# Attention's numerators in two single PSUM banks, and its output gates in three one-tile buffers

## The chip, the cores and the metric

The kernel runs on one core of a Trainium2 chip. The metric is the device time of one execution in microseconds (us). The engines are named as the profile names them: PE is TensorE (PEld its weight loads), DVE is VectorE, ACT is ScalarE, POOL is GpSimd, and SP is the engine whose queue issues the DMAs here.

## The reference

One layer of a hybrid decoder is computed for a prompt of 1024 new tokens and, beside it, for 8 sequences of 4 tokens each that go on from stored states. The branch that the change touches is an mLSTM with 4 heads of width 512, worked in chunks of 128 tokens:

```python
s = jnp.einsum('bhtd,bhsd->bhts', qc, kc) * d
num = jnp.einsum('bhts,bhse->bhte', s, vc) + g[..., None] * jnp.einsum('bhtd,bhde->bhte', qc, c)
den = jnp.sum(s, axis=-1) + g * jnp.einsum('bhtd,bhd->bht', qc, n)
h = num / jnp.maximum(jnp.abs(den), jnp.exp(-m_t))[..., None]
...
c_new = decay[..., None, None] * c + jnp.einsum('bhsd,bhse->bhde', kw, vc)
...
hc = hc.transpose(0, 2, 1, 3) * jax.nn.sigmoid(o_pre.astype(jnp.float32)).reshape(B, S, N_HEADS, HEAD_DIM)
hc = head_rmsnorm(hc, mlstm_norm_w).reshape(B, S, MLSTM_WIDTH).astype(x.dtype)
bm = (hc * jax.nn.silu(m_z)) @ w_mlstm_down
```

So each token tile's numerators are divided by a denominator, multiplied by the output gate `o`, normalised, and multiplied by a second gate `z`.

## The kernel before, in words

**Stages.** First the input projection of all heads is made, and q, k, v, the output gate (after its sigmoid) and z (after its silu) go to DRAM (`qkD`, `vD`, `oD`, `zD`). Then attention (`attn`) runs as a generator that is fed between the matmuls of the merge gates (`merge_gates`, whose products are the `mm` tiles). Behind it the decoding sequences (`sample`) run in the same way between the matmuls of the pooling branch, and the down projections (`downs`) and the tail end the kernel. Every fp32 product is made of three matmuls of a high and a low part (`mm3`, lines 383 to 385). A scheduler orders each engine's instructions: the first in program order that its own timing says is ready goes first. So matmuls of the merge gates, which stand among the steps of attention, fill waits of attention as long as there are any left.

**Attention** goes through 16 pairs of token tiles (4 heads of 4 pairs, numbered 0 to 15 here; pairs 0, 4, 8 and 12 are the first of a head, have no state yet and so fewer matmuls). For a pair the loads of `v`, `o` and `zz` (the gate z) bring 128 partitions x 2 tiles x 512 columns each, 512 KB, into one buffer for each of the three. For each of its two tiles:

- The numerators `num` are formed in two PSUM banks of one tile with one buffer: 256 columns of values in either bank, and in columns 256 and 257 of the first the denominator. The matmuls with the state's parts `Ch`, `Cl` go d by d, both banks for each d, and then those with the scores `ph`, `pl` and the values `vhi`, `vlo`.
- `attn_rows` reads them: ACT takes the denominator's absolute value (L1047), DVE makes its reciprocal (L1048, L1049), and DVE multiplies both banks by it and by `o`, in place of `o`, in one instruction of 512 columns (L1051). With that the banks are free. ACT sums the squares (L1054), the root is made on DVE and POOL (L391, L393), and DVE multiplies by it and by z (L1056).
- k is transposed and scaled into `kh`, `kl`.

Then the state C gets its update, 8 products `kv` in two PSUM buffers (L1025 or L1027 on DVE, then the split into `Ch`, `Cl`). The scores of the next pair are prepared among these (`attn_ahead`). At the pair's end `attn_turn` transposes both tiles of `o` on PE (L1063) and sends them off. Since `o` has one buffer, the next pair's `o` is loaded when these transposes are done; the buffer of `zz` is free when the second tile's L1056 is.

SP issues nearly all DMAs, in order: one that waits for its buffer holds those behind it.

Of the kernel before, what the change touches and what calls it, by code (L numbers as in the profile page):

```python
# [12 lines left out]
AF = mybir.ActivationFunctionType  # L13
ALU = mybir.AluOpType
# [4 lines left out]
P = 128  # L19
# [3 lines left out]
NS = DB * DS  # L23
NT = T + NS
H, DH = 4, 512
M = H * DH
KT = D // P
L = 128
# [312 lines left out]
class Trunk:  # L341
# [631 lines left out]
    def attn(self):  # L973

        nc = self.nc
        a = self.atp
# [3 lines left out]
        cut = lambda x: ((0, x[:, 0, :]), (1, x[:, 1, :256]))  # L980
        vh, vl = self.vhi, self.vlo
        for n, (h, j) in enumerate(pairs):
            qk, qh, ql, ph, pl = made
            both = lambda x: x[h][2 * j * L:(2 * j + 2) * L, :].rearrange("(i p) n -> p i n", p=P)
            r0 = h * NCH + 2 * j
            v, o, z = [self.t(a, [P, 2, 512], x) for x in ("v", "o", "zz")]
            for x, src in ((v, self.vD), (o, self.oD), (z, self.zD)):
                nc.sync.dma_start(x, both(src))
            khl = []
            for i in range(2):  # L990
                t = slice(i * L, (i + 1) * L)
                num = self.t(self.ps, [P, 2, 512], "num")
                outs = (num[:, 0, :258], num[:, 1, :256])
                if j:
                    for d in range(4):
                        for (x, mh), (_, ml) in zip(cut(self.Ch[:, d]), cut(self.Cl[:, d])):
                            self.mm3(outs[x], qh[:, d, t], ql[:, d, t], mh, ml, d == 0, False)
                v3 = v[:, i].rearrange("p (a n) -> p a n", a=2)
                self.hi(vh[i][:, :, 0:256], v3)
                self.lo(vl[i][:, :, 0:256], v3, vh[i][:, :, 0:256])  # L1000
                for b in range(i + 1):
                    c = slice((i + b) * L, (i + b + 1) * L)
                    for (x, mh), (_, ml) in zip(cut(vh[b]), cut(vl[b])):
                        self.mm3(outs[x], ph[:, c], pl[:, c], mh, ml, j == 0 and b == 0, b == i)
                yield True
                self.attn_rows(r0 + i, num, o[:, i], z[:, i])
                ps = self.miscps()
                for d in range(4):
                    nc.tensor.transpose(ps[:, d * P:(d + 1) * P], qk[:, 4 + d, t], self.ident)
                kh = self.t(a, [P, 4, P], f"kh{i}", F32R)  # L1010
                kl = self.t(a, [P, 4, P], f"kl{i}", F32R)
                ps3 = ps.rearrange("p (d f) -> p d f", d=4)
                w_s = self.tok[:, 1, r0 + i:r0 + i + 1]
                self.hi(kh, ps3, w_s)
                self.lo(kl, ps3, kh, w_s)
                khl.append((kh, kl))
                yield True
# [19 lines left out]
            for i in range(2):  # L1037
                self.attn_turn(h, 2 * j + i, o[:, i])
            if j == NCH // 2 - 1:
# [3 lines left out]
    def attn_rows(self, r, num, o, z):  # L1043

        nc, a = self.nc, self.atp
        den = self.t(a, [P, 1], "den", bufs=2)
        nc.scalar.activation(den, num[:, 0, 256:257], AF.Abs)  # L1047
        nc.vector.tensor_scalar(out=den, in0=den, scalar1=self.tok[:, 2, r:r + 1], scalar2=None, op0=ALU.max)  # L1048
        nc.vector.reciprocal(den, den)  # L1049
        o3 = o.rearrange("p (a n) -> p a n", a=2)  # L1050
        nc.vector.scalar_tensor_tensor(out=o3, in0=num[:, :, 0:256], scalar=den, in1=o3, op0=ALU.mult, op1=ALU.mult)  # L1051
        ss = self.t(a, [P, 1], "ss", bufs=2)
# [27 lines left out]
    def sample(self):  # L1080
# [57 lines left out]

        num = self.t(self.ps, [P, 2, 512], "num")
        qm = self.t(a, [P, 132 * DB], "qm")  # L1140
        nc.gpsimd.memset(qm, 0.0)
        for h in range(H):
# [19 lines left out]
            for b in range(DB):  # L1162
# [4 lines left out]
                for d in range(4):  # L1167
                    nc.tensor.matmul(num[32 * d:32 * d + 32, 0, :], lhsT=qm[:, b * P + d * NS:b * P + (d + 1) * NS], rhs=ct[:, d, :],  # L1168
                                     start=b == 0, stop=b == DB - 1)
# [8 lines left out]
            nsb = self.t(a, [P, DH], "voz", bufs=3)  # L1178
            nc.scalar.activation(nsb, num[:, 0, :], AF.Copy)
            nc.tensor.matmul(num[32 * h:32 * h + 32, 1, :], lhsT=self.sel, rhs=nsb, start=True, stop=False)  # L1180
        vo = []
        for src in (self.vSD, self.oSD, self.zSD):
            x = self.t(a, [P, DH], "voz", bufs=3)
            nc.sync.dma_start(x, src.rearrange("h t e -> (h t) e"))
            vo.append(x)
        nc.tensor.matmul(num[:, 1, :], lhsT=pb, rhs=vo[0], start=False, stop=True)
        hc = self.t(a, [P, DH], "shc")
        nc.vector.scalar_tensor_tensor(out=hc, in0=num[:, 1, :], scalar=dn, in1=vo[1], op0=ALU.mult, op1=ALU.mult)
        ss = self.t(a, [P, 1], "sss")
# [4 lines left out]
        for d in range(4):  # L1194
            nc.tensor.transpose(ps[:, d * P:(d + 1) * P], hc[:, d * P:(d + 1) * P], self.ident)
        for h in range(H):
            nc.vector.tensor_copy(self.hcS[:, h], ps.rearrange("p (d h t) -> p h d t", d=4, h=H)[:, h])
# [148 lines left out]
    def downs(self, first):  # L1346
# [35 lines left out]
        self.mmov = []  # L1382
        self.ms = self.t(self.cp, [P, KT, NS], "ms")
        for g in range(4):
# [163 lines left out]
    def run(self):  # L1548
# [50 lines left out]
        self.cp2, _c2 = self.pool("const2")  # L1599
        self.hcS = self.t(self.cp2, [P, H, 4, NS], "hcS")  # L1600
        self.wp, _w = self.pool("weights2")
# [77 lines left out]
```

## Time and profile before

| | |
|---|---|
| Median of 3 runs | 2232.88 us (2228.46 to 2236.81) |
| Profiled execution, its own time | 2232.33 us |
| Span of the profile (first to last instruction) | 2230.6 us |
| Mean granted clock of TensorE | 0.99 |
| Busy: PE / DVE / ACT / POOL | 97% / 56% / 40% / 6% |

The profile is of one execution. Idle time of an engine is put down to what released the instruction behind it. A granted clock of 1.00 is 2.4 GHz, and 0.50 is 1.2 GHz. Attention's matmuls start near 980 us of the span and end near 1345 us.

### The profile page before, as it was taken

To read this page: it belongs to the slowest core of one execution; us is meant where nothing else is said; L and a number is where in the kernel's file an instruction comes from. 1 tells how busy PE (TensorE), PEld (TensorE's weight loads), DVE (VectorE), ACT (ScalarE), POOL (GpSimd) and SP (SyncE) were. 2 spreads that over 40 slices of the span, in tenths; PEclk is the share of its full clock that TensorE was granted. 3 is DMA by queue.
4 is the path that set the end of the run, shared out by engine and by line. 5 is a ranking of instruction groups with operands and counts; after the bars stand their busy time and mean duration, and the time that the engine had idled before them with its cause. 6 is when DMAs were issued, how large, how long until landed. Compare 5 with 4: busy or idle time off the path is not lost.

```text
span 2230.6 us, 40176 instructions
## 1 busy us (share of the span) xinstructions
PE 2159.6 (97%) x16407; PEld 2054.8 (92%) x16407; DVE 1257.2 (56%) x2172; ACT 900.8 (40%) x1791; POOL 122.7 (6%) x335
## 2 busy tenths in 40 slices
PE   7999999999999999899999899999988999999998
PEld 6899999999999999899999798787778999999998
DVE  6855576456746565446566675576563243543645
ACT  5645455444635353633333343222223331213443
POOL 1100001000101000000000100000000000000000
PEclk9999999999999999999999999999999999999999
DMA  4233333333233331675655645887774343323112
GB/s 153 85 107 108 102 103 96 108 102 115 93 107 96 112 93 38 195 245 160 196 158 161 204 140 175 294 289 261 252 265 162 97 139 102 108 97 104 53 48 83
DMA packets 238601, 312.72 MB, mean 140 GB/s; under 512 B 13994, under 2 KB 170066, under 8 KB 238416
## 3 DMA queue, kind: packets, MB, share of 16 engines
q1 hardware_dynamic: 238416, 310.15, 42.8%
q8 instruction: 129, 2.11, 0.4%
q14 instruction: 56, 0.46, 0.1%
HBM read 200.01 MB, written 110.45 MB: 139 GB/s over the span
## 4 chain that ended last, share of the span: by engine, by line
PE 87%; DMA 6%; DVE 3%; ACT 2%; SPq 1%; issue 1%; POOL 0%; DVEq 0%; POOLq 0%; ACTq 0%
PE mm L221 21%; PE mm L163 14%; PE mm L383 12%; PE mm L385 12%; PE mm L384 12%; PE num L1168 2%; PE misc L953 2%; PE num L383 1%; PE kv L383 1%; PE num L384 1%; PE num L385 1%; PE kv L384 1%; PE kv L385 1%; PE kv L1172 1%; DMA o<-oD 1%; DMA ct<-state_mlstm_C 1%
## 5 line engine op out<-in xcount | busy, mean ns | idle before, releaser
L376 DVE TENSOR_TENSOR wlo<-wraw,whi 128x1024 fp32r<-128x1024 f32 (+1 forms) x220 | 238.7, 1086 | 228.7 <-ACT whi L370 222.9
L370 ACT ACTIVATE whi<-wraw 128x1024 fp32r<-128x1024 f32 (+1 forms) x220 | 209.2, 951 | 340.8 <-PE mm L221 107.1
L383 PE MATMUL mm<-hh,whi 128*128 128x352 f32 (+1 forms) x832 | 265.7, 319 | 14.5 <-ACT sz L1311 9.0
L385 PE MATMUL mm<-hh,wlo 128*128 128x352 f32 (+1 forms) x832 | 262.6, 316 | 0.0
L384 PE MATMUL mm<-hl,whi 128*128 128x352 f32 (+1 forms) x832 | 261.7, 315 | 0.0
L221 PE MATMUL mm<-wlo,hh 128*128 128x256 f32 x768 | 216.1, 281 | 0.0
L221 PE MATMUL mm<-whi,hl 128*128 128x256 f32 x768 | 215.9, 281 | 0.0
L221 PE MATMUL mm<-whi,hh 128*128 128x256 f32 x768 | 214.6, 279 | 0.0
L383 PEld LDWEIGHTS mm<-hh,whi 128*128 128x128 f32 x832 | 158.8, 191 | 28.5 <-ACT sz L1311 11.3
L384 PEld LDWEIGHTS mm<-hl,whi 128*128 128x128 f32 x832 | 159.2, 191 | 5.7 <-issue 4.4
L385 PEld LDWEIGHTS mm<-hh,wlo 128*128 128x128 f32 x832 | 158.7, 191 | 5.5 <-issue 4.2
L323 DVE SCALAR_TENSOR_TENSOR z<-z,vcols,z 128x556 f32<-128x556 f32 x192 | 146.8, 794 | 8.4 <-ACT z L321 6.6
L163 PE MATMUL mm<-hh,whi 128*128 128x264 f32 x512 | 148.4, 290 | 1.0 <-DVE z L179 0.6
L163 PE MATMUL mm<-hl,whi 128*128 128x264 f32 x512 | 146.2, 286 | 0.4 <-DVE hl L376 0.3
L163 PE MATMUL mm<-hh,wlo 128*128 128x264 f32 x512 | 145.5, 284 | 0.0
L221 PEld LDWEIGHTS mm<-whi,hh 128*128 128x128 f32 x768 | 144.7, 188 | 0.0
L221 PEld LDWEIGHTS mm<-whi,hl 128*128 128x128 f32 x768 | 144.6, 188 | 0.0
L221 PEld LDWEIGHTS mm<-wlo,hh 128*128 128x128 f32 x768 | 144.3, 188 | 0.2
L1173 DVE SCALAR_TENSOR_TENSOR ct<-ct,dec,kv 128x512 f32<-128x512 f32 x128 | 93.4, 744 | 70.9 <-PE kv L1172 61.3
L385 PE MATMUL mm<-mvhB,wlo 128*128 128x352 f32 x384 | 123.2, 322 | 0.0
L384 PE MATMUL mm<-mvlB,whi 128*128 128x352 f32 x384 | 123.0, 322 | 0.0
L383 PE MATMUL mm<-mvhB,whi 128*128 128x352 f32 x384 | 122.1, 324 | 0.0
(462 smaller groups left out, 6071.6 us busy)
## 6 DMA issues: line engine op xcount, KB each, us to landing
wraw<-w_in SPq DMA_DIRECT2D x112, 512.0 KB
ct<-state_mlstm_C SPq DMA_DIRECT2D x32, 1024.0 KB
new_C_sample<-ct SPq DMA_DIRECT2D x32, 1024.0 KB
qkD<-z SPq DMA_DIRECT2D x64, 256.0 KB
qk<-qkD SPq DMA_DIRECT2D x16, 1024.0 KB
sgD<-sz SPq DMA_DIRECT2D x16, 528.0 KB
sg<-sgD SPq DMA_DIRECT2D x16, 528.0 KB
vD<-z SPq DMA_DIRECT2D x32, 256.0 KB
```

Of the source, the lines that this page charges most:

```text
L163: self.tr.nc.tensor.matmul(ps[:, j, :CH], lhsT=st[:, k], rhs=mv[k][:, c], start=start and k == 0 and n == 0, stop=stop and k == 3 and n == ...
L221: self.tr.nc.tensor.matmul(ps[:, t // 2, t % 2 * 256:t % 2 * 256 + 256], lhsT=st[k][:, c], rhs=mv[:, k], start=start and t % 2 == 0 and k ...
L323: nc.vector.scalar_tensor_tensor(out=acc, in0=z[:, o:o + tot], scalar=wc(o), in1=acc, op0=ALU.mult, op1=ALU.add)
L370: self.nc.scalar.activation(out, in_, AF.Copy)
L376: self.nc.vector.tensor_tensor(out=out, in0=in_, in1=hi.bitcast(F32), op=ALU.subtract)
L383: mm(ps, lhsT=sh, rhs=mh, start=start, stop=False)
L384: mm(ps, lhsT=sh, rhs=ml, start=False, stop=False)
L385: mm(ps, lhsT=sl, rhs=mh, start=False, stop=stop)
L953: nc.tensor.matmul(out, lhsT=qk[:, 4 + d, i * L:(i + 1) * L], rhs=qk[:, d, i * L:], start=d == 0, stop=d == 3)
L1168: nc.tensor.matmul(num[32 * d:32 * d + 32, 0, :], lhsT=qm[:, b * P + d * NS:b * P + (d + 1) * NS], rhs=ct[:, d, :], start=b == 0, stop=b = ...
L1172: nc.tensor.matmul(kv, lhsT=km[:, d * P:(d + 1) * P], rhs=vst, start=True, stop=True)
L1173: nc.vector.scalar_tensor_tensor(out=ct[:, d, :], in0=ct[:, d, :], scalar=self.dec[:, h * DB + b, 1:2], in1=kv, op0=ALU.mult, op1=ALU.add)
```

## The change

The two PSUM banks of the numerators become two tiles, `num0` and `num1`, of one bank and one buffer each. All matmuls of a token tile into the first bank stand ahead of those into the second; the split of v stands ahead of both. L1051 becomes two instructions of 256 columns, one for each bank. The gate `o` is loaded by token tile, 256 KB at a time, into three buffers instead of one of two tiles; in program order the loads of a pair are now v, o, o, z. This takes 2 KB more of each partition. To make room, `hcS` (decoding's result) is written into the buffer of `ks` when decoding is done with it, and `ms` (a small copy for the tail) into that of `qs`. Decoding uses the same two banks, one tile for each.

```diff
-            v, o, z = [self.t(a, [P, 2, 512], x) for x in ("v", "o", "zz")]
-            for x, src in ((v, self.vD), (o, self.oD), (z, self.zD)):
-                nc.sync.dma_start(x, both(src))
+            o = [self.t(a, [P, 512], "o", bufs=3) for _ in range(2)]
+            v, z = [self.t(a, [P, 2, 512], x) for x in ("v", "zz")]
+            nc.sync.dma_start(v, both(self.vD))
+            for i in range(2):
+                nc.sync.dma_start(o[i], self.oD[h][(2 * j + i) * L:(2 * j + i + 1) * L, :])
+            nc.sync.dma_start(z, both(self.zD))
             khl = []
             for i in range(2):
                 t = slice(i * L, (i + 1) * L)
-                num = self.t(self.ps, [P, 2, 512], "num")
-                outs = (num[:, 0, :258], num[:, 1, :256])
-                if j:
-                    for d in range(4):
-                        for (x, mh), (_, ml) in zip(cut(self.Ch[:, d]), cut(self.Cl[:, d])):
-                            self.mm3(outs[x], qh[:, d, t], ql[:, d, t], mh, ml, d == 0, False)
                 v3 = v[:, i].rearrange("p (a n) -> p a n", a=2)
                 self.hi(vh[i][:, :, 0:256], v3)
                 self.lo(vl[i][:, :, 0:256], v3, vh[i][:, :, 0:256])
-                for b in range(i + 1):
-                    c = slice((i + b) * L, (i + b + 1) * L)
-                    for (x, mh), (_, ml) in zip(cut(vh[b]), cut(vl[b])):
-                        self.mm3(outs[x], ph[:, c], pl[:, c], mh, ml, j == 0 and b == 0, b == i)
+                num = []
+                for x in range(2):
+                    ps = self.t(self.ps, [P, 512], f"num{x}")
+                    num.append(ps)
+                    out = ps[:, :258 - 2 * x]
+                    if j:
+                        for d in range(4):
+                            self.mm3(out, qh[:, d, t], ql[:, d, t], cut(self.Ch[:, d])[x][1], cut(self.Cl[:, d])[x][1],
+                                     d == 0, False)
+                    for b in range(i + 1):
+                        c = slice((i + b) * L, (i + b + 1) * L)
+                        self.mm3(out, ph[:, c], pl[:, c], cut(vh[b])[x][1], cut(vl[b])[x][1], j == 0 and b == 0, b == i)
                 yield True
-                self.attn_rows(r0 + i, num, o[:, i], z[:, i])
+                self.attn_rows(r0 + i, num, o[i], z[:, i])
...
-        o3 = o.rearrange("p (a n) -> p a n", a=2)
-        nc.vector.scalar_tensor_tensor(out=o3, in0=num[:, :, 0:256], scalar=den, in1=o3, op0=ALU.mult, op1=ALU.mult)
+        for x in range(2):
+            o1 = o[:, x * 256:(x + 1) * 256]
+            nc.vector.scalar_tensor_tensor(out=o1, in0=num[x][:, 0:256], scalar=den, in1=o1, op0=ALU.mult, op1=ALU.mult)
...
+        self.hcS = self.t(self.cp, [P, H, 4, NS], "ks")
...
-        self.ms = self.t(self.cp, [P, KT, NS], "ms")
+        self.ms = self.t(self.cp, [P, KT, NS], "qs")
...
-        self.hcS = self.t(self.cp2, [P, H, 4, NS], "hcS")
```

SP's order at the loads of pairs 11 and 12, before (`o_14018`, `zz_14019` and `v_14017` are of pair 11, `qk_14247` of pair 12; `hcD` takes the transposed `o` of pair 10):

```order
L988 DMA v_14017<-vD_7_66 128x2x512
L988 DMA zz_13784<-zD_15_74 128x2x512
L988 DMA o_13783<-oD_11_70 128x2x512
L1066 DMA hcD_19_78<-t2k_13779 512x1x128
L941 DMA qk_14247<-qkD_4_63 128x8x256
L1066 DMA hcD_19_78<-t2k_14006 512x1x128
L943 DMA dg_14249<-DD_1258_11114 128x384
L988 DMA zz_14019<-zD_15_74 128x2x512
L988 DMA o_14018<-oD_11_70 128x2x512
```

And now (`zz_13844` is of pair 10; `o_14082` and `o_14083` are the two tiles of pair 11, with `v_14084` and `zz_14085`; `o_14410` is the first tile of pair 12):

```order
L991 DMA zz_13844<-zD_15_74 128x2x512
L990 DMA o_14082<-oD_11_70 128x512
L1072 DMA hcD_19_78<-t2k_13838 512x1x128
L941 DMA qk_14318<-qkD_4_63 128x8x256
L988 DMA v_14084<-vD_7_66 128x2x512
L990 DMA o_14083<-oD_11_70 128x512
L943 DMA dg_14320<-DD_1257_11113 128x384
L1072 DMA hcD_19_78<-t2k_14071 512x1x128
L991 DMA zz_14085<-zD_15_74 128x2x512
L990 DMA o_14410<-oD_12_71 128x512
```

The first tile's `o` has moved from behind its own pair's `zz` to behind that of the pair before; the second tile's stands behind `v`; `zz` has kept its place ahead of the other pair's `o`.

PE's order where the second tile of pair 10 begins, before (one tile `num_13843`, 258 columns in the first bank and 256 in the second):

```order
L385 MATMUL kv_13912<-vhi_1263_11130,kl_1737_13901 128x256
L383 MATMUL num_13843<-Ch_11140,qh_13702 128x258
L384 MATMUL num_13843<-Cl_11141,qh_13702 128x258
L385 MATMUL num_13843<-Ch_11140,ql_13703 128x258
L383 MATMUL num_13843<-Ch_11140,qh_13702 128x256
L384 MATMUL num_13843<-Cl_11141,qh_13702 128x256
L385 MATMUL num_13843<-Ch_11140,ql_13703 128x256
```

And now, at the change from its first bank (`num_1760_13908`) to its second (`num_1761_13927`):

```order
L385 MATMUL num_1760_13908<-vhi_1261_11128,pl_13768 128x258
L383 MATMUL num_1760_13908<-vhi_1262_11129,ph_13767 128x258
L384 MATMUL num_1760_13908<-vlo_1264_11131,ph_13767 128x258
L385 MATMUL num_1760_13908<-vhi_1262_11129,pl_13768 128x258
L383 MATMUL num_1761_13927<-Ch_11139,qh_13761 128x256
L384 MATMUL num_1761_13927<-Cl_11140,qh_13761 128x256
L385 MATMUL num_1761_13927<-Ch_11139,ql_13762 128x256
```

All 18 matmuls of the first bank are now ahead of the 18 of the second; before, the banks took turns by three.

PE's order where the last matmuls of the merge gates (`mm`) stand among those of attention, before, in pair 8 (`num_13286` and `num_13317` are its two tiles):

```order
L385 MATMUL num_13286<-vhi_1262_11129,pl_13204 128x256
L383 MATMUL mm_15487<-hh_135,whi_15456 128x352
L384 MATMUL mm_15487<-hl_136,whi_15456 128x352
L385 MATMUL mm_15487<-hh_135,wlo_15457 128x352
L1009 MATMUL misc_13308<-ident_112,qk_13188 128x128 x4
L1009 MATMUL misc_13345<-ident_112,qk_13188 128x128 x4
L383 MATMUL num_13317<-vhi_1262_11129,ph_13203 128x258
```

And now, in pair 9 (`num_1702_13530` and `num_1703_13546` are the two banks of its first tile, `kv_13494` is still of pair 8):

```order
L385 MATMUL kv_13494<-vhi_1262_11129,kl_1677_13404 128x256
L383 MATMUL num_1702_13530<-Ch_11139,qh_13440 128x258
L383 MATMUL num_1703_13546<-Ch_11139,qh_13440 128x256
L384 MATMUL mm_15583<-hl_136,whi_15552 128x352
L385 MATMUL mm_15583<-hh_135,wlo_15553 128x352
L384 MATMUL num_1702_13530<-Cl_11140,qh_13440 128x258
L385 MATMUL num_1702_13530<-Ch_11139,ql_13441 128x258
```

The filler now ends most of a pair later. The total of its matmuls is the same.

## Rows read from the trace of the kernel before

**Rows 1.** Head of the page: span, busy time of each engine and share of the span.

```profile
span 2230.6 us, 40176 instructions
...
PE 2159.6 (97%) x16407; PEld 2054.8 (92%) x16407; DVE 1257.2 (56%) x2172; ACT 900.8 (40%) x1791; POOL 122.7 (6%) x335
```

**Rows 2.** Busy time by stretches: stretch and length, busy us (count), clock, DMA share, GB/s.

```profile
980.00:1187.00 207.00, 207.00 (x1532) 205.03 (x1531) 122.41 (x235) 80.10 (x160) 9.67 (x16) 1.00 0.55 171
1187.00:1345.20 158.20, 145.64 (x1083) 137.82 (x1081) 110.75 (x227) 64.14 (x134) 13.00 (x19) 0.97 0.53 168
```

**Rows 3.** Waits of PE, 1187 to 1345.2 us: total us, times, longest.

```profile
PE num L383 <- DVE o L1051: 7.8, 5, 2.5
```

**Rows 4.** Waits of DVE, 1187 to 1345.2 us.

```profile
DVE o L1051 <- DMA o<-oD: 14.2, 6, 4.5
```

**Rows 5.** Timeline of PE in pairs 8, 10, 12, 15: start, length; idle before in brackets.

```profile
1194.40 0.36 PE L383 MATMUL num<-vhi,ph 128*128 128x258 f32 x1 [2.14 <-DVE o L1051]
...
1239.35 0.39 PE L383 MATMUL num<-Ch,qh 128*128 128x258 f32 x1 [1.98 <-DVE o L1051]
...
1278.56 0.36 PE L383 MATMUL num<-vhi,ph 128*128 128x258 f32 x1 [2.51 <-DVE o L1051]
...
1281.88 1.09 PE L1063 MATMUL misc<-ident,o 128*128 128x128 f32 x4 [1.64 <-issue]
...
1335.13 0.36 PE L383 MATMUL num<-Ch,qh 128*128 128x258 f32 x1 [1.01 <-DVE o L1051]
```

**Rows 6.** Chain of waits ahead of the same four places: start and length of each load.

```profile
1187.83 5.54 DMA o<-oD
...
1231.44 7.00 DMA o<-oD
...
1269.61 7.96 DMA o<-oD
...
1329.26 4.85 DMA o<-oD
```

**Rows 7.** Busy time by stretches, columns as in rows 2.

```profile
1195.00:1198.50 3.50, 3.50 (x20) 3.50 (x18) 1.85 (x6) 0.23 (x2) 0.55 (x1) 0.54 0.74 254
1280.00:1287.00 7.00, 5.36 (x26) 5.17 (x26) 5.58 (x12) 2.69 (x5) 1.00 (x1) 0.51 0.21 70
1287.00:1290.00 3.00, 3.00 (x27) 3.00 (x26) 2.96 (x8) 1.96 (x5) 0.73 (x1) 1.00 0.36 89
1236.00:1240.00 4.00, 2.02 (x17) 1.79 (x16) 0.75 (x1) 0.63 (x2) 0.00 (x0) 1.00 1.04 364
1305.00:1330.00 25.00, 24.75 (x196) 23.90 (x196) 21.20 (x43) 13.82 (x28) 2.00 (x3) 1.00 0.38 111
```

**Rows 8.** Timeline of SP: issue of the `zz` loads of pairs 10 and 12.

```profile
1230.73 0.37 SPq L988 DMA_DIRECT2D zz<-zD  x1
...
1269.01 0.51 SPq L988 DMA_DIRECT2D zz<-zD  x1
```

**Rows 9.** Timeline of DVE in pair 10.

```profile
1231.16 0.16 DVE L1049 RECIPROCAL den<-den 128x1 f32<-128x1 f32 x1
...
1238.54 0.75 DVE L1051 SCALAR_TENSOR_TENSOR o<-num,den,o 128x512 f32<-128x512 f32 x1 [4.21 <-DMA o<-oD]
...
1241.91 0.75 DVE L1056 SCALAR_TENSOR_TENSOR o<-o,rs_r,zz 128x512 f32<-128x512 f32 x1 [0.44 <-POOL rs_r L393]
```

**Rows 10.** Timeline of DVE in pair 12.

```profile
1281.03 0.75 DVE L1056 SCALAR_TENSOR_TENSOR o<-o,rs_r,zz 128x512 f32<-128x512 f32 x1 [0.44 <-POOL rs_r L393]
...
1293.09 1.40 DVE L378 SCALAR_TENSOR_TENSOR kl<-misc,tok,kh 128x512 fp32r<-128x512 f32 x2
```

**Rows 11.** Groups of DVE by line and shape, 1187 to 1345.2 us: busy, mean ns.

```profile
L1051 DVE SCALAR_TENSOR_TENSOR o<-num,den,o 128x512 f32<-128x512 f32 x16 | 12.0, 748 | 14.6 <-DMA o<-oD 14.2 <-PE kv L385 0.4
...
L1027 DVE SCALAR_TENSOR_TENSOR C<-C,dec,kv 128x256 f32<-128x256 f32 x24 | 11.4, 474 | 0.3 <-PE kv L385 0.3
```

**Rows 12.** Waits of PE in the decoding stage, 1345.2 to 1760 us.

```profile
PE num L1168 <- DMA ct<-state_mlstm_C: 6.0, 4, 3.7
```

More of the change, by code (lines that the diff above doesn't have):

```diff
@@ L1037, in attn @@
             for i in range(2):
-                self.attn_turn(h, 2 * j + i, o[:, i])
+                self.attn_turn(h, 2 * j + i, o[i])
             if j == NCH // 2 - 1:
@@ L1046, in attn_rows @@
         den = self.t(a, [P, 1], "den", bufs=2)
-        nc.scalar.activation(den, num[:, 0, 256:257], AF.Abs)
+        nc.scalar.activation(den, num[0][:, 256:257], AF.Abs)
         nc.vector.tensor_scalar(out=den, in0=den, scalar1=self.tok[:, 2, r:r + 1], scalar2=None, op0=ALU.max)
         nc.vector.reciprocal(den, den)
-        o3 = o.rearrange("p (a n) -> p a n", a=2)
-        nc.vector.scalar_tensor_tensor(out=o3, in0=num[:, :, 0:256], scalar=den, in1=o3, op0=ALU.mult, op1=ALU.mult)
+        for x in range(2):
+            o1 = o[:, x * 256:(x + 1) * 256]
+            nc.vector.scalar_tensor_tensor(out=o1, in0=num[x][:, 0:256], scalar=den, in1=o1, op0=ALU.mult, op1=ALU.mult)
         ss = self.t(a, [P, 1], "ss", bufs=2)
@@ L1136, in sample @@
         nc.sync.dma_start(O["new_n_sample"].rearrange("b h d -> (b h) d"), nt)
-        num = self.t(self.ps, [P, 2, 512], "num")
+        num = [self.t(self.ps, [P, 512], f"num{x}") for x in range(2)]
         qm = self.t(a, [P, 132 * DB], "qm")
@@ L1167, in sample @@
                 for d in range(4):
-                    nc.tensor.matmul(num[32 * d:32 * d + 32, 0, :], lhsT=qm[:, b * P + d * NS:b * P + (d + 1) * NS], rhs=ct[:, d, :],
+                    nc.tensor.matmul(num[0][32 * d:32 * d + 32], lhsT=qm[:, b * P + d * NS:b * P + (d + 1) * NS], rhs=ct[:, d, :],
                                      start=b == 0, stop=b == DB - 1)
@@ L1178, in sample @@
             nsb = self.t(a, [P, DH], "voz", bufs=3)
-            nc.scalar.activation(nsb, num[:, 0, :], AF.Copy)
-            nc.tensor.matmul(num[32 * h:32 * h + 32, 1, :], lhsT=self.sel, rhs=nsb, start=True, stop=False)
+            nc.scalar.activation(nsb, num[0], AF.Copy)
+            nc.tensor.matmul(num[1][32 * h:32 * h + 32], lhsT=self.sel, rhs=nsb, start=True, stop=False)
         vo = []
@@ L1185, in sample @@
             vo.append(x)
-        nc.tensor.matmul(num[:, 1, :], lhsT=pb, rhs=vo[0], start=False, stop=True)
+        nc.tensor.matmul(num[1], lhsT=pb, rhs=vo[0], start=False, stop=True)
         hc = self.t(a, [P, DH], "shc")
-        nc.vector.scalar_tensor_tensor(out=hc, in0=num[:, 1, :], scalar=dn, in1=vo[1], op0=ALU.mult, op1=ALU.mult)
+        nc.vector.scalar_tensor_tensor(out=hc, in0=num[1], scalar=dn, in1=vo[1], op0=ALU.mult, op1=ALU.mult)
         ss = self.t(a, [P, 1], "sss")
```

## The prediction

> **What bounds the kernel now.** The head of the page comes first: TensorE is busy for 97% of a span of 2230.6 us, so the change can give back only what TensorE stands idle, or runs at the lower clock, in the stages that it touches [rows 1]. The view of busy time by stretches splits attention in two: from 980 to 1187 us TensorE is busy in all 207.00 us, because the scheduler fills its waits with matmuls of the merge gates; from 1187 to 1345.2 us that filler is used up, and it is busy in 145.64 of 158.20 us, at a mean clock of 0.97 [rows 2]. These are pairs 8 to 15, and only there can a shorter wait be worth time.
>
> Which wait ends last there is read from the waits of TensorE and of VectorE. TensorE's largest item is the numerators' first matmul waiting for L1051, 7.8 us; VectorE in turn waits at L1051 for the load of `o`, 14.2 us in 6 waits [rows 3, 4]. The timeline of TensorE gives the places: 2.14 us before 1194.40 (pair 8, call it A), 1.98 before 1239.35 (pair 10, B), 2.51 before 1278.56 and 1.64 before 1281.88 (pair 12, C), 1.01 before 1335.13 (pair 15, D) [rows 5]. The chain of waits shows the same step at all four: the transposes of the pair before release the `o` buffer, the load takes 5.54, 7.00, 7.96 and 4.85 us, then L1051 reads the numerators and frees the bank [rows 6].
>
> Two places cost more than their idle time, since the granted clock fell behind them to 1.2 of 2.4 GHz: 0.54 on average from 1195 to 1198.5 us, and 0.51 from 1280 to 1287 us [rows 7]. In the first, 3.50 busy us at 0.54 hold 1.6 us too many. In the second, 26 matmuls took 5.36 us, where right behind it 27 took 3.00, so 2.5 us too many.
>
> So the wait on `o` costs A 2.14 + 1.6 = 3.7 us, B 2.0, C 2.51 + 1.64 + 2.5 = 6.7 and D 1.0, together 13.4 us.
>
> **The change part by part.** *Three buffers of one tile each for `o`.* Pair n takes two of the three; the load for the first tile of pair n+1 needs the buffer that the second tile of pair n-1 left, so in SP's order it stands right behind the `zz` load of pair n, a whole pair ahead of its use. The load for the second tile waits for the transposes of the first tile of pair n, and is used one tile later. The wait of L1051 on `o` should go at all of A to D: 13.4 us at most.
>
> *What is late next: z.* `zz` still has one buffer of two tiles and is loaded when L1056 of the pair's second tile has read it, as now. At B it was issued at 1230.73 and at C at 1269.01 [rows 8], 0.7 and 0.6 us ahead of `o` (1231.44 and 1269.61 [rows 6]), on the same queue and of the same 512 KB. So I put its landing ahead of that of `o` by at least this lead, and by at most the time of 512 KB at the 364 GB/s of that stretch, 1.4 us [rows 7]. At B `o` landed at 1238.44, hence z at 1237.0 to 1237.7. The denominator's reciprocal was ready at 1231.3; L1051 came at 1238.54 and L1056 3.37 us behind it, at 1241.91 [rows 9]. After the change the two halves of L1051 can run at 1231.3, and L1056 would be due near 1234.9: VectorE, which works in order, will stand at L1056 for 2 to 3 us instead of 4.21 at L1051. Behind L1056 are queued the updates of C and the split of the next q, and TensorE's kv banks wait for the former. But both numerator banks are free by then, so TensorE has the second tile's numerators (36 matmuls) and kv work to go on with, and I count B in full.
>
> At C this is different. Its pair is a head's first, with only 18 numerator matmuls, and TensorE reaches the transposes of `o` early: that is the 1.64 us. `o` landed at 1277.57, so z between 1276.2 and 1277.0, and L1056 moves from 1281.03 by 4.0 to 4.8 us; from there VectorE is almost without a pause busy until the last `kl` of 1293.09 [rows 10], at which TensorE takes up the next kv. So C is worth what VectorE moves, I take 4.5 of its 6.7 us; its bounds are 2.5 (if only the idle time at the bank goes) and 6.7.
>
> A counts in full, 3.7: in the new order TensorE's filler lasts into pair 9 instead of ending in pair 8, so there is work to stand in for a late z. D counts 1.0. Sum of gains: 3.7 + 2.0 + 4.5 + 1.0 = 11.2 us.
>
> *L1051 in two halves.* One took 748 ns at 512 columns. No half exists before; the nearest row is L1027, the same operation with a numerator-like PSUM operand at 256 columns, 474 ns [rows 11]. Two are 948, so 0.2 us more VectorE time for each tile, or 0.4 for a pair. The bounds are 0 (the first half runs while TensorE forms the second bank) and two whole ones, 0.75 more. In the steady pairs it is hidden: from 1305 to 1330 us VectorE was busy in 21.20 of 25 us while TensorE had 24.75 [rows 7]; without that slack it would be 16 x 0.2 = 3.2 us. Only around C, where VectorE paces, do I count it: two tiles, 0.4 us.
> The Trainium skill (VectorE: DVE Perf Modes, The TRN2 errata) speaks against such a cut: an instruction pays a fixed cost, so tiles should have 512 elements or more. Its cycle figures for a PSUM source give, as an estimate, 658 ns and twice 392, so 0.13 us more for a tile and 0.3 us at C instead of 0.4; the trace's own rows are longer on both sides, and the sum goes by them.
>
> *One bank behind the other.* The same matmuls and weight loads, so nothing on TensorE itself. The denominator stands in the first bank, so it is made while TensorE fills the second, and the next tile's first bank is free sooner. This shortens the release after the last matmul, which stands free of a load only at small waits; bounds 0 and what is left of the 7.8 us once the four places are taken out, 0.2; I take 0.
>
> *One more load for each pair, `hcS` and `ms` in old buffers.* An issue takes SP 0.37 us [rows 8], and in these pairs SP waits for buffers; 0. The moved buffers are written long after their last reader; 0.
>
> *Order.* From attention on the scheduler's order shifts a little, in the decoding stage behind it too, where TensorE waited 6.0 us for the state's loads [rows 12]. No row tells which way this goes; I count 0, with half of that wait, 3 us, to either side, and 0.3 us for new small waits.
>
> **Sum.** 11.2 - 0.4 - 0.3 = 10.5 us. The profiled execution took 2232.33 us, its span and 1.7 us around it; it is 0.55 below the median of 2232.88, well within that median's own runs (2228.46 to 2236.81). 2232.3 - 10.5 = 2221.8, so 2222 us.
>
> **Rivals.** *z takes the place of `o`.* For it: same queue, same size, issued only 0.6 and 0.7 us earlier at C and B, and VectorE works in order. Against it: z holds no bank. If TensorE runs dry behind it at A and C as it does now, what is left is B, D and A's 2.14: 5 us, so 2227.
> *All of it comes back.* If VectorE makes up its time at C, the whole 13.4 us return, and with the filler's longer reach a few small waits of that stretch (it has 12.56 idle us in all): 14 us, so 2218. Against it: VectorE's unbroken work behind 1281.03.
> *The loads are not earlier.* SP works in order too: if the second tile's load waits long for its transposes, `zz` and the next `o` stand behind it. Then one wait is exchanged for another: 2232. Against it: these transposes come before the L1056 on which `zz` waits anyway.
> *Slower.* VectorE becomes the bound. It has 3.8 us of slack in 25 us, so 2.9 us in a pair of 19; the halves take 0.4. If z, behind one half load of `o` more, holds VectorE for over 2.5 us in every pair, each further us costs 8 us in all; at 5 us of hold that is 20 us, less 11 given back: 9 us more, 2241. Against it: z is issued before `o` now and not later than now after the change, since all that stands ahead of it in SP's queue is free earlier than its own buffer; and in the steady pairs, 1305 to 1330 us, TensorE had 24.75 of 25 us [rows 7] with these loads as late as they are.
>
> **How the numbers follow.** Chances: forecast 0.46 (own range 2218 to 2226), z in place of `o` 0.20, all of it 0.19, loads not earlier 0.08, slower 0.07. A measurement of this kernel can tell about 0.5%, 11.2 us, so the line for faster is at 2221.7, in the middle of the forecast. Faster: 0.19 and somewhat over half of the forecast, 0.45. Slower 0.08, within 0.5% the rest, 0.47. The range takes in the full return with 3 us of luck in the later stage (2213) and the unchanged case with 2 us against it (2234); what lies outside is mostly the slower case.
>
> **What would show it.** Right: L1051's halves do not wait for `o` (14.2 us now), TensorE's waits on them fall below 2 us, no stretch near 0.5 of the clock at A and C, and busy time between the filler's end and attention's end is over 96% of it, against 92%. VectorE waits 2 to 3 us at L1056 for `zz` at B and C. A half of L1051 takes about 0.47 us. Wrong: idle time of TensorE before the `o` transposes or the kv matmuls as long as it had at the bank; the clock falling at new places; a loss in the decoding stage of over 3 us.

## The result, and the profile after

The changed kernel takes 2219.65 us (median of 4 runs, 2218.51 to 2220.86), the kernel before 2231.74 us in the runs taken beside it (4 runs, 2228.46 to 2236.81): a ratio of 0.9944, 95% interval 0.9926 to 0.9961, so 12.1 us faster. 2222 was forecast, with 2213 to 2234 as the range.

The head of the page of the changed kernel, and its busy time by stretches (columns as in rows 2; the second stretch ends where attention now ends, the third is the decoding stage):

```profile
span 2218.3 us, 40279 instructions
...
PE 2156.1 (97%) x16407; PEld 2051.3 (92%) x16407; DVE 1264.6 (57%) x2204; ACT 901.1 (41%) x1791; POOL 121.3 (5%) x335
```

```profile
980.00:1187.00 207.00, 207.00 (x1538) 205.01 (x1538) 128.72 (x257) 82.27 (x165) 10.50 (x16) 1.00 0.57 178
1187.00:1331.30 144.30, 140.54 (x1082) 134.73 (x1080) 112.33 (x237) 62.58 (x130) 9.77 (x17) 1.00 0.55 172
1331.30:1760.00 428.70, 407.43 (x2577) 344.76 (x2578) 229.38 (x467) 129.34 (x260) 17.55 (x58) 0.98 0.67 232
```

Between the filler's part and the end of attention TensorE was busy in 145.64 of 158.20 us at a clock of 0.97 [rows 2]; now in 140.54 of 144.30, at 1.00 throughout. The stretch is 13.9 us shorter.

TensorE's waits after the change from 1187 to 1331.9 us (total us, times, longest), which answer to [rows 3], and below them the largest of VectorE's, which answer to [rows 4]:

```profile
PE kv L383 <- DVE C L1030: 1.1, 1, 1.1
PE misc L1069 <- DVE o L1062: 0.7, 2, 0.4
PE misc L1095 <- ACT t2k L1071: 0.6, 1, 0.6
PE kv L384 <- DVE vlo L376: 0.5, 1, 0.5
PE kv L383 <- DVE C L1032: 0.5, 1, 0.5
PE misc L1014 <- ACT t2k L1071: 0.4, 1, 0.4
```

```profile
DVE o L1062 <- POOL rs_r L393: 6.0, 9, 0.7
DVE C L1032 <- PE kv L385: 4.8, 8, 1.7
DVE den L1053 <- ACT den L1052: 4.0, 10, 0.8
DVE C L1030 <- PE kv L385: 3.3, 4, 1.4
DVE qk L958 <- PE misc L953: 3.2, 3, 2.5
DVE o L1057 <- PE num L385: 2.7, 4, 1.0
```

The 7.8 us of TensorE at the numerators and the 14.2 us of VectorE at `o` are gone, and nobody waits for `zz` either.

How long attention is as a whole can be read from two groups of instructions in each kernel, by the start of their first and last: the first numerator (`num<-vhi,ph`), and the last transposes of `o`. Before, and then after (durations in ns, then first and last start in us):

```profile
L383 PE MATMUL num<-vhi,ph x96: 278/283/472, 979.9 to 1339.2; 128*128 128x258 f32 x48, 128*128 128x256 f32 x48
L1063 PE MATMUL misc<-ident,o x128: 270/272/448, 992.6 to 1344.8; 128*128 128x128 f32 x128
```

```profile
L383 PE MATMUL num<-vhi,ph x96: 278/284/470, 980.8 to 1326.8; 128*128 128x258 f32 x48, 128*128 128x256 f32 x48
L1069 PE MATMUL misc<-ident,o x128: 270/272/311, 992.8 to 1330.9; 128*128 128x128 f32 x128
```

Attention takes 350.1 us now and took 364.9: 14.8 us less. From there to the end of the span it is 887.4 us against 885.8, 1.6 more, and the first numerator starts 0.9 later; together 12.3, the difference of the spans.

### The profile page after: what moved, and what is told of

Same layout as the page of the kernel before. It is cut to its first block, busy times and chain, and to the rows that moved or that the text cites. A ratio compares the mean times of both kernels' runs of the same rounds, so it can differ in the third digit from the quotient of the medians.

```text
span 2218.3 us, 40279 instructions
## 1 busy us (share of the span) xinstructions
PE 2156.1 (97%) x16407; PEld 2051.3 (92%) x16407; DVE 1264.6 (57%) x2204; ACT 901.1 (41%) x1791; POOL 121.3 (5%) x335
## 4 chain that ended last, share of the span: by engine, by line
PE 88%; DMA 5%; DVE 3%; ACT 1%; SPq 1%; issue 1%; DVEq 0%; POOLq 0%; ACTq 0%
PE mm L221 21%; PE mm L163 15%; PE mm L383 12%; PE mm L385 11%; PE mm L384 11%; PE misc L953 2%; PE num L1174 2%; PE num L384 1%; PE num L383 1%; PE num L385 1%; DMA ct<-state_mlstm_C 1%; PE kv L383 1%; PE kv L384 1%; PE kv L385 1%; PE kv L1178 1%; PE misc L736 1%
## 5 line engine op out<-in xcount | busy, mean ns | idle before, releaser
L376 DVE TENSOR_TENSOR wlo<-wraw,whi 128x1024 fp32r<-128x1024 f32 (+1 forms) x220 | 238.8, 1085 | 231.2 <-ACT whi L370 228.0
```

Of the source, the lines that this page charges most:

```text
L376: self.nc.vector.tensor_tensor(out=out, in0=in_, in1=hi.bitcast(F32), op=ALU.subtract)
```

## The experiments

All times are medians beside runs of the kernel before on the same chip. "Attention" is the time between the starts above (in two kernels to the last kv matmul, which there stands behind the transposes), "behind" is the rest of the span.

| kernel | us (runs) | ratio (95%) | attention | behind |
|---|---|---|---|---|
| before | 2230.7 to 2232.9 in four series | 1 | 364.9 | 885.8 |
| changed, again (`e4`) | 2219.30 (5) | 0.9940 (0.9928 to 0.9952) | 350.0 | 886.8 |
| loads of `o` alone (`e1`) | 2236.85 (11) | 1.0020 (1.0010 to 1.0030) | 358.7 | 893.7 |
| split alone (`e2`; `e5`) | 2223.98 (11; a twelfth is told of in the last section); 2222.31 (9) | 0.9964 (0.9951 to 0.9976); 0.9962 (0.9947 to 0.9976) | 353.8 (`e5`) | 890.0 |
| changed, `o` in two buffers (`e3`) | 2221.32 (6) | 0.9944 (0.9930 to 0.9958) | 350.7 | 890.2 |
| split alone, banks in turns (`e8`) | 2224.98 (10) | 0.9973 (0.9961 to 0.9985) | 354.8 | 888.0 |
| joint banks, one behind the other (`e9`) | 2241.62 (6) | 1.0039 (1.0019 to 1.0059) | 372.2 | 883.4 |
| changed, banks in turns (`e10`) | 2219.04 (4) | 0.9947 (0.9926 to 0.9968) | 350.1 | 887.3 |
| changed, L1057 in quarters (`e11`) | 2217.51 (4) | 0.9935 (0.9910 to 0.9960) | 351.0 | 886.8 |
| loads of `o` and of z (`e12`) | 2233.77 (10) | 1.0007 (0.9996 to 1.0018) | 357.9 | 892.6 |

### One part at a time

The first series took the two halves of the change apart. The kernel before with the loads alone:

```diff
-            v, o, z = [self.t(a, [P, 2, 512], x) for x in ("v", "o", "zz")]
+            o = [self.t(a, [P, 512], "o", bufs=3) for _ in range(2)]
+            v, z = [self.t(a, [P, 2, 512], x) for x in ("v", "zz")]
...
                 num = self.t(self.ps, [P, 2, 512], "num")
...
```

> The kernel before with the loads of o alone changed (by token tile, three buffers, with the room made for it); the numerators stay one tile of two banks, and L1051 one instruction of 512 columns. Theory, the early loads of o are all of the gain: 2218 to 2222 us, VectorE's wait for the load of o gone (14.2 us before), no stretch of attention at half the clock. Rival, the split banks carry a good part (the first bank is free earlier): 2223 to 2228 us with TensorE's numerators still waiting 3 us or more for L1051. Rival, the gain is a shifted order of the scheduler: anything, with the filler not reaching into pair 9.

It came out slower than before, 2236.85 us, which neither the theory nor the first rival had expected. The second rival left the time open, and its sign is there: the filler ends in pair 8 as before, while in the changed kernel it reaches into pair 9. These are the last matmuls of the merge gates in this kernel and in the changed one:

```profile
1192.26 0.33 PE L385 MATMUL mm<-hh,wlo 128*128 128x352 f32 x1
```

```profile
1205.88 0.32 PE L385 MATMUL mm<-hh,wlo 128*128 128x352 f32 x1
```

Attention did get 6.2 us shorter, though 3.4 us of it still run at half the clock (1264.97 to 1268.38 us). VectorE waits for no `o`, but it now waits for the load named in the first rival of the prediction (VectorE's waits, 1187 to 1340 us), and the stages behind attention lost 7.9 us, about what TensorE waits more at the state's loads (its waits, 1340 to 1760 us; 6.0 us before [rows 12]; the mean clock of that stretch is 0.96, before it was 0.98):

```profile
DVE o L1059 <- DMA zz<-zD: 4.4, 3, 1.9
...
PE num L1171 <- DMA ct<-state_mlstm_C: 14.5, 5, 6.0
```

The changed kernel with the old loads, so the split alone:

```diff
-            o = [self.t(a, [P, 512], "o", bufs=3) for _ in range(2)]
-            v, z = [self.t(a, [P, 2, 512], x) for x in ("v", "zz")]
...
+            v, o, z = [self.t(a, [P, 2, 512], x) for x in ("v", "o", "zz")]
...
```

> The changed kernel with the old loads of o (one buffer of two tiles); only the numerators' split and the moved small buffers are left. Theory, the early loads of o are all of the gain: 2230 to 2235 us, VectorE still waits 12 to 16 us for o between 1187 us and the end of attention, TensorE still stands idle at the numerators behind it. Rival, the split carries a good part: 2222 to 2227 us, TensorE fills the wait with the second bank.

> The kernel with the numerators' split alone once more, for a trace of an undisturbed execution: the profiled execution of the first run took 7387 us and says nothing of its stages. 2219 to 2231 us, as the other eleven executions. Theory, the split lets TensorE work on while VectorE waits for o: VectorE still waits 10 us or more for o, but TensorE's idle time at the numerators from 1187 us to the end of attention is under 4 us, against 7.8, and the clock does not fall there. Rival, the split moves the scheduler's order, and the gain lies in the decoding stage: attention ends less than 4 us earlier than before, and decoding is shorter by 4 us or more.

The theory that the loads are all of the gain fell: the split alone is 8 us faster than before, and its attention is 11.1 us shorter, with `o` still loaded late. VectorE's waits for `o` from 1187 us to attention's end are less than half of [rows 4], and TensorE's at the numerators are a ninth of [rows 3]:

```profile
DVE o L1054 <- DMA o<-oD: 6.2, 3, 3.2
```

```profile
PE num L383 <- DVE o L1054: 0.9, 1, 0.9
```

Of the two ways in which `e5` could end, neither holds as it was put: TensorE's idle time did fall below 4 us there, but so did VectorE's wait for a load that the edit hadn't touched.

> The changed kernel with two one-tile buffers of o in place of three. The load for a pair's first tile then waits for the transposes of the first tile of the pair before, and not a whole pair ahead. Theory, what counts is that a tile's load does not wait for the second tile's transposes: most of the gain stays, 2219 to 2224 us, with waits of VectorE for o of 0 to 4 us. Rival, the third buffer is what takes the load out of the way: 2226 to 2232 us, with 8 us or more of waits for o.

> The changed kernel itself, on the chip of the three runs above: 2218 to 2221 us, and its trace again without a wait for o or zz.

With two buffers of `o` attention takes 350.7 us, and VectorE waits for `o` once, 0.8 us. The third buffer, for which 2 KB of each partition were freed, carries no time that these runs can tell. The changed kernel repeated its time and its trace.

### Why the split shortens a wait for a load

The SP timeline of the split alone gives the reason. These are the issues of `o` for pairs 10, 11 and 12, and VectorE at L1054 (the halves) in pairs 10 and 11:

```profile
1223.63 0.37 SPq L988 DMA_DIRECT2D o<-oD  x1
1240.80 0.36 SPq L988 DMA_DIRECT2D o<-oD  x1
1260.19 0.44 SPq L988 DMA_DIRECT2D o<-oD  x1
```

```profile
1229.16 0.88 DVE L1054 SCALAR_TENSOR_TENSOR o<-num,den,o 128x256 f32<-128x256 f32 x2 [1.72 <-DMA o<-oD]
...
1250.52 0.88 DVE L1054 SCALAR_TENSOR_TENSOR o<-num,den,o 128x256 f32<-128x256 f32 x2
```

In pair 11 the load is issued 9.7 us ahead of its use, and is on time though it is still a late load of 512 KB. In pair 10 before, the load was issued at 1231.44 [rows 6], when the denominator had already been ready [rows 9]; here it is issued 5.5 us before L1054 runs. The scheduler has put the transposes that release `o` earlier in TensorE's order. Counted in the program's order, from the last of a pair's transposes to the end of the next pair's first numerator bank, in matmuls (negative: the transposes stand behind it), for the loads of pairs 8 to 15:

| kernel | lead in matmuls | attention |
|---|---|---|
| before | 18, 79, -7, 26, 8, 26, 26, 26 | 364.9 |
| split alone | 51, 83, 23, 57, 9, 39, 23, 49 | 353.8 |
| split alone, banks in turns | 30, 75, 25, 25, 19, 25, 25, 25 | 354.8 |
| joint banks, one behind the other | 12, 45, -19, 20, 8, 20, 20, 20 | 372.2 |

The changed kernel has the same leads as the split alone; TensorE's order is the same in both all through attention. So 353.8 against 350.1, 3.7 us, is what the early loads give when the order is held.

The last two kernels were made to tell the order from the early release of a bank. In the third, tiles and halves are as in the change, the loads of `o` are the old ones, and the matmuls take turns as before:

```diff
...
-                for x in range(2):
-                    ps = self.t(self.ps, [P, 512], f"num{x}")
...
+                num = [self.t(self.ps, [P, 512], f"num{x}") for x in range(2)]
+                outs = (num[0][:, :258], num[1][:, :256])
+                if j:
+                    for d in range(4):
+                        for (x, mh), (_, ml) in zip(cut(self.Ch[:, d]), cut(self.Cl[:, d])):
+                            self.mm3(outs[x], qh[:, d, t], ql[:, d, t], mh, ml, d == 0, False)
...
```

> The numerators in two tiles of one bank each and L1051 in halves, the old loads of o, but the matmuls of both banks taking turns d by d as before. In TensorE's order the transposes that release o stand 30, 75, 25, 25, 19, 25, 25, 25 matmuls ahead of the end of the next pair's first bank, in pairs 8 to 15 (before 18, 79, -7, 26, 8, 26, 26, 26; with the split alone and its banks one behind the other 51, 83, 23, 57, 9, 39, 23, 49). Theory, this lead is what the split changes: waits for o vanish in pairs 8, 10 and 12 for the most part, attention ends 7 to 10 us earlier than before, 2222 to 2227 us. Rival, it is the early release of the first bank that the one behind the other gives: attention ends less than 4 us earlier, 2229 to 2233 us.

In the fourth, one tile of two banks stays, and only the order of the text changes (the split of v moves ahead of both banks, as in the change):

```diff
...
+                num = self.t(self.ps, [P, 2, 512], "num")
+                outs = (num[:, 0, :258], num[:, 1, :256])
+                for x in range(2):
+                    if j:
+                        for d in range(4):
+                            self.mm3(outs[x], qh[:, d, t], ql[:, d, t], cut(self.Ch[:, d])[x][1], cut(self.Cl[:, d])[x][1],
+                                     d == 0, False)
...
```

> The kernel before with one thing changed: all matmuls into the first bank ahead of those into the second, but in one tile of two banks as before, with L1051 whole and the old loads of o. The lead of the transposes over the end of the next pair's first bank in TensorE's order is 12, 45, -19, 20, 8, 20, 20, 20 matmuls, less than before. Theory of the lead: no gain, VectorE waits 14 to 20 us for o between 1187 us and attention's end, 2232 to 2238 us. Rival, the order of the matmuls into the banks brings the gain of the split: 2222 to 2228 us.

`e8` took the time that the theory of the lead gave (2224.98 us, attention 10.1 us shorter), but not its waits: VectorE still waits 10.7 us for `o`, in 7 pieces, and in pairs 8, 10 and 12 it waits 2.31, 1.23 and 3.33 us, where it was 1.95, 4.21 and 4.47. Only pair 10 lost most of its wait. In pair 8 the wait costs TensorE nothing, because it has other matmuls there, the filler's among them: it is busy in 17.79 of the 18.00 us from 1187 to 1205. These are VectorE's wait in pair 8 and the filler's last matmul in `e8`, and the filler's last before:

```profile
1192.92 0.88 DVE L1052 SCALAR_TENSOR_TENSOR o<-num,den,o 128x256 f32<-128x256 f32 x2 [2.31 <-DMA o<-oD]
...
1199.05 0.32 PE L385 MATMUL mm<-hh,wlo 128*128 128x352 f32 x1
```

```profile
1191.06 0.33 PE L385 MATMUL mm<-hh,wlo 128*128 128x352 f32 x1
```

`e9` was slower, as the theory of the lead said, and by more than its numbers: 2241.62 us, attention 7.3 us longer. But longer waits for `o` are not the reason: they are 11.8 us, where 14 to 20 were expected and 14.2 were there before. What grew is VectorE's wait for the denominators, and TensorE stands at more places (waits from 1187 us to attention's end; VectorE's before, and then `e9`):

```profile
DVE den L1048 <- ACT den L1047: 14.6, 10, 3.3
```

```profile
DVE den L1048 <- ACT den L1047: 22.0, 9, 4.8
...
PE num L383 <- DVE o L1051: 5.7, 4, 2.5
PE misc L1063 <- DVE o L1056: 3.1, 6, 0.7
PE kv L383 <- DVE C L1027: 2.0, 4, 1.4
PE kv L383 <- DVE C L1025: 1.8, 2, 1.0
```

So putting one bank behind the other is no gain by itself; it came with a loss where the banks are released together, and with separate tiles it matters little whether the banks take turns. What came with the split is another order, in which the old load is less late and the filler lasts longer. That this order is the reason is argued from the traces and not shown: no run holds the order and splits the tile alone. The edit of `e8` in the changed kernel asks whether the lead is needed once `o` is early:

> The changed kernel with the early loads of o and two tiles, but both banks' matmuls taking turns d by d. Theory, with o early no lead is needed, so the order of the banks counts for little: 2218 to 2224 us, no wait for o. Rival, one behind the other is worth something by itself, since the second bank covers the denominator: 2225 to 2230 us, with TensorE waiting for the bank at L1057 for 4 us or more.

2219.04 us and 350.1 us of attention, as with the banks one behind the other. It is not needed.

### Where z lands, and whether it took the place of `o`

One GpSimd copy of a column of z, in the kernel before and in the changed one, shows its landing (one run each, 2228.86 and 2220.50 us):

```diff
+            nc.gpsimd.tensor_copy(self.t(a, [P, 1], "pz", bufs=2), z[:, 0, 0:1])
```

> The kernel before with one GpSimd copy of one column of each pair's z into a scratch tile, which waits for the load of z and so shows when it lands. The prediction put z's landing at 1276.2 to 1277.0 us in pair 12, 7.2 to 8.0 us behind its issue, and 6.3 to 7.0 us behind it in pair 10. Theory, z shares the queue with o and lands just ahead of it: 6 to 8 us. Rival, z takes 5 us or less: then it could not have been late.

> The changed kernel with the same copy of one column of z. Theory, without the second load of 512 KB behind it z lands in 4 to 5.5 us after its issue, ahead of the second gate's first use. Rival, it takes 6 us or more as before, and is only issued earlier against its use.

The issue and the landing in pair 12, before and then after the change, and in the latter the use by VectorE:

```profile
1271.68 0.41 SPq L988 DMA_DIRECT2D zz<-zD  x1
...
1278.68 0.18 POOL L989 COPY pz<-zz 128x1 f32<-128x1 f32 x1 [8.65 <-DMA zz<-zD]
```

```profile
1260.03 0.40 SPq L991 DMA_DIRECT2D zz<-zD  x1
...
1265.65 0.18 POOL L992 COPY pz<-zz 128x1 f32<-128x1 f32 x1 [7.49 <-DMA zz<-zD]
...
1266.47 0.75 DVE L1063 SCALAR_TENSOR_TENSOR o<-o,rs_r,zz 128x512 f32<-128x512 f32 x1 [0.73 <-POOL rs_r L393]
```

Before, z took 7.0 us, just under the 7.2 to 8.0 of the prediction, and 6.4 in pair 10, within its 6.3 to 7.0. After, it takes 5.6 (theory: 4 to 5.5; rival: 6 or more; 5.2 in pair 10), and lands 0.8 us ahead of the use, which waits for GpSimd's root until then anyway. z is therefore next in line, and just not late.

In the kernel with the loads of `o` alone it was late, three times. The last experiment loads z by tile there, in two buffers, with TensorE's order the same to the last matmul:

```diff
-            v, z = [self.t(a, [P, 2, 512], x) for x in ("v", "zz")]
+            v = self.t(a, [P, 2, 512], "v")
+            z = [self.t(a, [P, 512], "zz", bufs=2) for _ in range(2)]
...
```

> The kernel with the early loads of o alone (numerators in one tile of two banks), and z by token tile too, in two buffers of one tile; TensorE's order is the same to the last matmul as with o alone. There attention, from its first numerator to its last transposes of o, took 358.8 us against 365.0 before and 350.1 in the changed kernel, and VectorE waited 4.4 us for z in 3 waits. Theory, z has taken the place of o there: attention takes 354 to 357 us without these waits. Rival, the order alone holds it back: 358 to 359 us. For the stage behind: if its longer waits for the state (14.5 us against 6.0 before) come from the order of the instructions, they are 12 us or more again, and the kernel takes 2230 to 2236 us; if they were chance, 5 to 8 us and 2222 to 2228 us.

VectorE's waits for z are gone, but attention takes 357.9 us, 0.8 less than without: the theory fell, and what is left is the rival, that the order holds that kernel back. TensorE's largest waits there hang on no gate load (1187 us to attention's end):

```profile
PE misc L1068 <- DVE o L1061: 2.1, 1, 2.1
PE num L383 <- ACT ph L370: 2.1, 1, 2.1
PE num L383 <- DVE o L1056: 1.1, 3, 0.8
```

So with no gate load late in either, the joint tile still takes 7.8 us longer than the changed kernel (350.1). A load that is less late can't be all that the split is worth; which waits the rest lies in was not taken apart.

Behind attention the same order gave nearly the same loss again, 892.6 us, and TensorE waits for the state's loads:

```profile
PE num L1173 <- DMA ct<-state_mlstm_C: 11.7, 7, 4.2
```

That is just short of the 12 us that were set for "the order does it", and far from the 5 to 8 of "chance".

### The price of cutting L1051

```diff
-        for x in range(2):
-            o1 = o[:, x * 256:(x + 1) * 256]
+        for x in range(4):
+            o1 = o[:, x * 128:(x + 1) * 128]
+            c = x % 2 * 128
```

> The changed kernel with L1057 in four instructions of 128 columns instead of two of 256. From 748 and 481 ns for 512 and 256 columns I estimate 347 ns for 128, so 1.39 us for a tile instead of 0.96, twice the price of the cut that the change made. Theory, VectorE has room for it: attention ends at most 1.5 us later, 2218 to 2223 us. Rival, VectorE is at its limit in these pairs: 16 x 0.43 = 7 us or more later, 2226 us or above.

Groups of VectorE by line and shape, the halves in the changed kernel and the quarters here (busy us, mean ns):

```profile
L1057 DVE SCALAR_TENSOR_TENSOR o<-num,den,o 128x256 f32<-128x256 f32 x30 | 13.7, 481 | 4.0 <-PE num L385 2.7
```

```profile
L1058 DVE SCALAR_TENSOR_TENSOR o<-num,den,o 128x128 f32<-128x128 f32 x64 | 18.7, 346 | 3.7 <-PE num L385 2.2
```

Two halves cost 962 ns against 748 whole [rows 11], four quarters 1384; attention is 0.9 us longer and the kernel not slower (2217.51 us). VectorE has room for twice the cut, though it now waits 1.0 us for z once, which it did not with the halves. TensorE's order differs there too, so the 0.9 us are not the price of the cut alone. The Trainium skill (VectorE: DVE Perf Modes, The TRN2 errata) advises tiles of 512 elements or more for the fixed cost of an instruction; the fixed cost is there in these rows (267 ns for the columns from 256 to 512, 135 from 128 to 256, which leaves some 210 that hang on no column), and the kernel was not slower for it.

## Why the prediction was right, point by point

**The places.** That the change could give back only TensorE's idle and half-clock time behind the filler held: from 1187 us to attention's end TensorE's idle time fell by 8.8 us (12.56 to 3.76), where the places have 9.3, and its busy time by 5.1, where the half clock was put at 4.1. The two sides of each place can be set beside each other by the reciprocal of a pair's first denominator: pair 10 at 1231.16 before [rows 9] and 1227.89 after, pair 12 at 1272.31 and 1263.99 (timelines of VectorE; the first row is of before, the other two of after):

```profile
1272.31 0.16 DVE L1049 RECIPROCAL den<-den 128x1 f32<-128x1 f32 x1
```

```profile
1227.89 0.17 DVE L1054 RECIPROCAL den<-den 128x1 f32<-128x1 f32 x1
...
1263.99 0.15 DVE L1054 RECIPROCAL den<-den 128x1 f32<-128x1 f32 x1
```

Up to pair 10 the kernel gained 3.3 us, and 4.2 counted from the first numerator, where 3.7 were counted for A. From pair 10 to pair 12 it is 36.1 us instead of 41.1, so 5.0 against the 2.0 of B. From pair 12 to the last transposes (1344.8 and 1330.9) it is 66.9 instead of 72.5: 5.6, where C, D and the halves were put at 4.5 + 1.0 - 0.4 = 5.1. Attention in all: 14.8 against 10.8.

**The term that was mis-sized is B.** In that stretch TensorE was idle for 3.74 of 41.1 us before (37.36 busy) and is for 0.5 of 36.1 now: besides the 1.98 at the bank some 1.3 us of small waits at other steps went as well. The other 1.8 us are busy time, at a clock of 1.00 in both; 9 matmuls fewer start between the two marks (284 and 275), which is a part of it, and the rest was not traced. The small waits are what the case "all of it comes back" had in it; its 14 us are what attention gave. The time of the whole kernel, 2219.65, lies between that case's 2218 and the forecast's 2222 and doesn't tell them apart; attention does.

**z.** VectorE was to stand at L1056 for 2 to 3 us in pairs 10 and 12. It doesn't wait for z there at all. The step that failed is z's landing as taken over from the old traffic. There it was right, but now z takes 5.2 us in pair 10 and 5.6 in pair 12 instead of 6.4 and 7.0, and its use comes 7.3 and 6.4 us behind its issue (the kernel with the copy); for pair 10 the prediction had it due 4.2 us behind (1230.73 to 1234.9). So the 2.2 us by which C was marked down rest on a wait that did not come. In the kernel with the loads alone it did come, 4.4 us in all, with 1.91 us in pair 10 and 0.61 in pair 12 smaller than described.

**One bank behind the other, taken at 0, and the order, taken at 0.** Both terms failed as reasons, and that the total came out all the same is luck to that extent. The loads were credited with all of A to D, but alone they shorten attention by 6.2 us and leave the kernel 0.2% slower; the split, whose bounds were 0 and 0.2, shortens it by 11.1 alone. On top of the other edit the loads give 3.7 and the split 8.6 (358.7 to 350.1). The two don't add up (17.3 against 14.8): 2.5 us come with either edit, which fits a wait that the one removes by an earlier load and the other by an order in which the old load is less late. The 8.6 need another reason, as `e12` shows. Had only one of the two edits been forecast by the same sum, it would have failed.

**The halves.** 481 ns against the row of 474 that was used, hidden in VectorE's slack as counted.

**The stage behind.** Nothing was counted, with 3 us to either side; 1.6 us were lost, within that. Its length was 880.6 to 893.7 us over all kernels here, and 885.8 and 880.6 for before and its copy with the probe, whose TensorE order is the same: 5 us can be chance of one execution. The loss of 7 to 8 us with the loads of `o` alone came twice with one order of TensorE, and it is there in the medians too: with attention's change taken off the change of the median, 10.4 us are left for `e1` and 7.9 for `e12`, and -0.5 to 3.2 for the others. The waits at the state's loads are the largest piece of it that the traces show. Which instruction of that order makes them late was not settled.

**Slower** was put down to a VectorE at its limit; the quarters show that it is not. A slower kernel was near all the same, through the order: half of this very change is one.

## What to carry to other kernels

Where a scheduler places the instructions, an edit that only splits a tile can come with another order, and in this kernel that was worth more than the transfer made earlier beside it (11.1 us of attention against 6.2, each alone); print the order and count the work between the release and the use before giving such an edit a price of nothing. When two edits attack one wait, run each alone: their gains overlap, and one of them may be a loss by itself. A buffer freed with trouble, as the third one here, is worth a run without it.

## What the hardware showed that was not expected

One execution of the split alone (`e2`), the one that was profiled, took 7387 us; the other eleven took 2219 to 2231. Its page shows TensorE busy throughout, with a group of matmuls of 128x352 (and one other form) at a mean of 776 ns where the changed kernel has 318, while VectorE's and ScalarE's instructions kept their durations (1086 and 948 ns against 1085 and 951). Here the group in that trace and in the changed kernel's:

```profile
L383 PE MATMUL mm<-hh,whi 128*128 128x352 f32 (+1 forms) x832 | 645.8, 776 | 5.3 <-ACT sz L1315 2.7
```

```profile
L383 PE MATMUL mm<-hh,whi 128*128 128x352 f32 (+1 forms) x832 | 264.5, 318 | 14.3 <-ACT sz L1318 8.4
```

What clock TensorE was granted there is not known: the trace of `e2` holds no records of it, its page alone lacks the row of the granted clock, and the 1.00 that the views print for it is what they print where records are missing. So look whether the records are there before reading a granted clock; the mean of one form of matmul does not need them. The slow execution did not come again in the other runs, and its cause is open.
